# A down projection regrouped: 4 plain chunks, then five groups of a chained 7-product scheme

## The chip, the cores and the metric

The kernel runs on one core of a Trainium2 chip. The metric is the device time of one execution in microseconds (us). A core has TensorE (PE in the profile, with PEld for its weight loads), VectorE (DVE), ScalarE (ACT), GpSimd (POOL) and a queue engine, SyncE (SP), that issues most DMAs. The kernel before took 3144.01 us (median of 3 runs, 3142.61 to 3148.22).

## What is computed

One layer of a hybrid encoder for 640 tokens (512 of a prompt, 8 x 16 of running streams): norm, a combined input projection, gated DeltaNet and sliding-window attention, an output projection, then a ConvFFN. The change touches only the last product:

```python
h2 = rms_norm(x, norm2_w) * (1 + scale2) + shift2
u = h2 @ w_up                                  # 2048 -> 2 x 5632
u_c = causal_dwconv(concat(ffn_prev, u), ffn_conv_w) + ffn_conv_b
gt, up = split(u_c, 2)
x = x + gate2 * ((silu(gt) * up) @ w_down)     # 5632 -> 2048
```

All of it is float32. gate2 is one vector for the prompt and one for each of the 8 streams.

## The kernel before

Features lie on the partitions in chunks of 128, tokens along the free axis: 640 columns in two halves of 320 (HALF), each with 256 columns of the prompt and 64 of four streams. The inner width of 5632 is 44 chunks (NFF), the output 2048 is 16 rows of 128 (KC).

A float32 product is built from three matmuls: each operand x is split into hi (x rounded to float32r, a copy on ACT) and lo = x - hi (a subtraction on DVE), and hi x hi, hi x lo and lo x hi are summed in PSUM. This holds for weights (tiles raw, whi, wlo of 128x512, a unit of four 128x128 blocks) and for activations.

Weights come as a stream of units in a fixed order, which `build_stream` writes down. SP fetches 512 KB at a time into a ring of five buffers (`issue_raw`), `prep_next` forms the sum or difference of two units where one is wanted (tile wsum, a ring of three), `split_next` makes whi and wlo (rings of four), and `next_unit` keeps four units prepared ahead of PE (UB) and the sums two units ahead of those (skew).

Where a group is split, a block product with 2 x 2 blocks (two halves of the features, two halves of the output rows, two halves of the tokens) is made from seven products instead of eight, in ORDER. One job is one value of f, the output rows f and f + 8 together: 7 products of 4 chunks each, 12 matmuls of 320 columns a product. Operand sums are made of weights (five of seven products need one; DPOOL says which GpSimd makes) and of tokens (`mixes`, once a group). The products' sums are formed outside PE: `down(f)` reads every product from PSUM with ACT or DVE, combines them on DVE and GpSimd, and `resid` adds each of the four results to the resident y: one scalar_tensor_tensor on DVE for the 256 prompt columns with gate2, one product into rst on DVE and one addition on GpSimd for the 64 others.

The down projection's 44 chunks go in groups, DGRP: plain 4, split 8, plain 4, split 8, plain 4, split 8, plain 8. In a plain group each of the 16 rows f gets 6 matmuls a chunk (both token halves) and two calls of `resid`. After the last group each row is stored.

Banks: `next_bank` hands out four banks in turn from two PSUM tiles of two banks, named mmd (even) and mm (odd): tile 0 bank 0, tile 1 bank 0, tile 0 bank 1, tile 1 bank 1.

The order of all instructions is written at build time, and every engine runs its own in that order. `Model` keeps an estimated clock for each engine; a side task is a generator in a `Lane`, and `tick`, called after every three or six matmuls, lets lanes go on as long as what they need is ready by that clock. The filling of token operands for the down projection is lane "c" (`chunks`). The gated activations go through DRAM (md): stored by SP chunk by chunk in the up projection, loaded again by GpSimd's queue. The convolution of a pair of up rows is a list of steps that are handed out at SLOTS within the next pair's products; the last pair's come within the first plain group.

Every instruction is recorded at line 90, the wrapper that accounts it, so tiles and not lines tell the operations apart.

Of the kernel before, what the change touches and what calls it, by code (L numbers as in the profile page):

```python
# [6 lines left out]
F32 = mybir.dt.float32  # L7
# [9 lines left out]
ORDER = (2, 4, 5, 1, 6, 7, 3)  # L17
NF = 8
# [14 lines left out]
DGRP = ((0, 4), (1, 8), (0, 4), (1, 8), (0, 4), (1, 8), (0, 8))  # L33
EARLY = 2
DPOOL = {2: 0, 5: 1, 1: 1, 6: 0, 7: 1}
DMIXP = (0, 1, 1, 0, 1)
# [58 lines left out]
class Model:  # L95
    """Estimates when each engine and each tile is free, to order the instructions of parallel tasks."""
# [79 lines left out]
class Ring:  # L176
    """Slots taken in turn, each a tag of a pool."""
# [18 lines left out]
class Slots:  # L196
    """Tiles of any width up to n in the slots of a ring."""
# [30 lines left out]
class Kern:  # L228
# [66 lines left out]
    def add_unit(self, h, *srcs, op=None, pool=False):  # L295
        """Half h (one for all or one each) of one source, or of the sum or difference of two."""
        self.units.append(([k for k, _ in srcs], h if isinstance(h, tuple) else (h,) * len(srcs), op, pool))
        for k, ap in srcs:
            if k not in self.rleft:
                self.rorder.append((k, ap))  # L300
                self.rleft[k] = 0
            self.rleft[k] += 1
# [6 lines left out]
    def build_stream(self):  # L309
# [26 lines left out]
        for split, m in DGRP:  # L336
            for u in range(0 if split else 4 * m):
                self.add_unit(u % 2, (("d", n + u // 2), d["wdn"][n + u // 2]))
            for f in range(8 if split else 0):
                for p in ORDER:  # L340
                    o = OPER[p]
                    src = [(("d", n + 2 * f + j), d["wdn"][n + 2 * f + j]) for j, _ in o[:2]]
                    self.add_unit(tuple(r for _, r in o[:2]), *src, op=o[2] if len(o) > 2 else None, pool=DPOOL.get(p))
            n += 2 * m
# [9 lines left out]
    def prep_next(self):  # L354
        self.issue_raw()
        keys, h, op, pool = self.units[self.apos]
        src = [self.rtile[k][:, i * 512:(i + 1) * 512].rearrange("p (k m) -> p k m", k=4) for k, i in zip(keys, h)]
        if op is not None:
            e = self.nc.gpsimd if pool else self.nc.vector
            t = self.rsum.take([P, 4, P], F32, "wsum")  # L360
            e.tensor_tensor(out=t, in0=src[0], in1=src[1], op=op)
            src = [t]
            self.release(keys)
            keys = ()
        self.ltile[self.apos] = src[0], keys
        self.apos += 1
# [28 lines left out]
    def mm_quarter(self, ps, unit, acts, first, last):  # L395
        nc = self.nc
        hi, lo = unit
        for k, (xh, xl) in enumerate(acts):
            for i, (w, x) in enumerate(((hi, xh), (hi, xl), (lo, xh))):
                nc.tensor.matmul(out=ps, lhsT=w[:, k, :], rhs=x, start=first and k == 0 and i == 0,  # L400
                                 stop=last and k == len(acts) - 1 and i == 2)
# [1050 lines left out]
    def mix_start(self):  # L1452
        """The last gate and the first block of the output projection, as their operands come."""
# [58 lines left out]
    def head(self, h):  # L1512
        """Convolved queries and keys of head h; calling the result gives them with the values."""
# [28 lines left out]
    def phase2(self):  # L1542
# [4 lines left out]
        self.md = tc.dram_tile([NFF, P, NT], F32, name="md")  # L1547
        self.pd = tc.dram_tile([NP, 4, P, HALF], F32, name="pd")
        with tc.tile_pool(name="xres", bufs=1, reuse_waits="tile") as xr, \
# [20 lines left out]
            with tc.tile_pool(name="opx", bufs=1, reuse_waits="tile") as ox:  # L1570
# [3 lines left out]
                with tc.tile_pool(name="ffn", bufs=1, reuse_waits="tile") as fp:  # L1574
                    self.ffn(Tiles(nc, fp, 1))

    def attn_out(self, pa, load):
        """Output projection with its residual, norm, and the first products of NP pairs."""
# [87 lines left out]
    def operand(self, p, j):  # L1666
        """Token operand of product p for the features of chunks j and j + 8, as a sum of two parts."""
# [34 lines left out]
    def pipe(self, ks, ops, s=0, rB=None):  # L1702
        """Steps that scale rows ks, then make the operands ops, a stage of it a step."""
# [45 lines left out]
    def product(self, p, step=None, nh=2):  # L1749
        ps = self.next_bank()  # L1750
        for h in range(nh):
            un = self.next_unit()
            self.feed(self.rate)
            for k in range(4):
                while len(self.ops[p]) <= 4 * h + k:
                    if self.bg:
                        self.feed()
                    else:
# [3 lines left out]
                self.mm_quarter(ps, (un[0][:, k:k + 1], un[1][:, k:k + 1]), [x], h == 0 and k == 0,  # L1762
                                h == nh - 1 and k == 3)
# [4 lines left out]
    def ffn(self, fp):  # L1768
# [18 lines left out]
        def up(i):  # L1787
# [9 lines left out]
            for q, pr in enumerate(ORDER):  # L1797
# [26 lines left out]
                if i == NFF - 1 and q == 3:  # L1824
                    self.lanes["c"].add(chunks())
# [76 lines left out]
        acts, ops, raws, ap, ox = {}, {}, [], self.ap, self.ox  # L1902
        stag = [(ap, f"a{x}{k}") for k in range(6, 16) for x in "hl"] + [(ox, f"ex{k}") for k in range(8)]
        spare = Ring(None, "", 0)
        spare.slots = [[ap, f"a{x}{k}", None] for k in (4, 5) for x in "hl"]
        sums = Slots(spare, NT)

        def raw(c):
            tag = ("ftm", "fext")[len(raws) // 2 % 2]
            raws.append(c)  # L1910
            t = fp.tile([P, 658], F32, tag=tag, name="mraw", bufs=2)[:, 0:NT]
            nc.gpsimd.dma_start(out=t, in_=self.md[c])
            return t

        def whole(c, s, t):
            """Both parts of chunk c, in slot s."""
            tags = [(ap, f"a{x}{s}") for x in "hl"] if s < 4 else stag[2 * s - 8:2 * s - 6]
            hi, lo = (p.tile([P, NT], F32R, tag=n, name=f"m{x}") for x, (p, n) in zip("hl", tags))
            yield (t,)
            nc.scalar.copy(out=hi, in_=t)  # L1920
            yield (hi,)
            v.tensor_tensor(out=lo, in0=t, in1=hi.bitcast(F32), op=ALU.subtract)
            acts[c] = (hi, lo)
            self.done.add(("m", c))

        def mixes(c0, fetch):
            """Token operands of all products for chunks c0 .. c0 + 7, a stage of several at a time."""
            todo, src, hi, low = [(k, q) for k in range(4) for q in range(7)], {}, {}, {}
            for n in range(len(todo) + 3):
                if n < 28:  # L1930
                    k, q = todo[n]
                    if q == 0:
                        while k + 2 > EARLY and self.steps:
                            yield
                        b = [[t[:, s * HALF:(s + 1) * HALF] for s in range(2)] for t in fetch[k]()]
                        (b11, b12), (b21, b22) = b
                        expr = {2: (b11,), 5: (b22,), 4: (b21, b11, ALU.subtract), 1: (b11, b22, ALU.add),
                                6: (b11, b12, ALU.add), 7: (b21, b22, ALU.add), 3: (b12, b22, ALU.subtract)}
                        yield b21, b11
                    x = expr[ORDER[q]]  # L1940
                    src[n] = x[0]
                    if len(x) > 1:
                        src[n] = sums.tile([P, HALF], F32, "", "msum")
                        e = nc.gpsimd if DMIXP[q - 1 - (q > 2)] else v
                        e.tensor_tensor(out=src[n], in0=x[0], in1=x[1], op=x[2])
                if 0 <= n - 1 < 28:
                    k, q = todo[n - 1]
                    yield (src[n - 1],)
                    pool, tag = stag[4 * q + k]
                    t = pool.tile([P, NT], F32R, tag=tag, name="mop")  # L1950
                    hi[n - 1], low[n - 1] = t[:, 0:HALF], t[:, HALF:NT]
                    nc.scalar.copy(out=hi[n - 1], in_=src[n - 1])
                m = n - 2
                if 0 <= m < 28:
                    yield (hi[m],)
                    v.tensor_tensor(out=low[m], in0=src[m], in1=hi[m].bitcast(F32), op=ALU.subtract)
                    ops[c0][ORDER[todo[m][1]]].append((hi[m], low[m]))

        def chunks():
            c0, ts = 0, []  # L1960
            for c in range(4):
                ts.append(ap.tile([P, NT], F32, tag=f"ah{c + 8}", name="mraw"))
                nc.gpsimd.dma_start(out=ts[c], in_=self.md[c])
            for g, (split, m) in enumerate(DGRP):
                if split:
                    ops[c0] = {p: [] for p in ORDER}
                    rs, early = [], EARLY if g == 1 else 0

                    def get(k):
                        if k < early:  # L1970
                            rs.append([stag[18 - 4 * k + j][0].tile([P, NT], F32, tag=stag[18 - 4 * k + j][1], name="mraw")
                                       for j in range(2)])
                            for j in range(2):
                                nc.gpsimd.dma_start(out=rs[k][j], in_=self.md[c0 + k + 4 * j])
                        else:
                            rs.append((raw(c0 + k), raw(c0 + k + 4)))

                    for k in range(max(1, early)):
                        get(k)

                    def fetch(k):
                        while len(rs) < min(k + 2, 4):
                            get(len(rs))
                        return rs[k]

# [216 lines left out]
```

## Time and profile before

| | |
|---|---|
| timed runs | 3142.61, 3144.01, 3148.22 us |
| profiled execution, first to last instruction (span) | 3137.7 us; its time with what lies around the span isn't shown |
| PE busy | 2974.9 us, 95%, 19841 matmuls |
| DVE busy | 2319.3 us, 74% |
| ACT busy | 1195.7 us, 38% |
| GpSimd busy | 1147.2 us, 37% |
| DMA | 428.32 MB, 137 GB/s on average |
| mean granted clock of TensorE | 0.983 of 2.4 GHz |

Busy time is the union of an engine's instructions. Matmuls are pipelined: a row gives 0.31 us for a matmul of 320 columns, but the next one starts before that is over, so the pace is read from start to start or from many in a row. The same holds for DVE: an operation's duration is some 0.08 us longer than the distance to the start of the next. The up projection fills PE from about 1600 us to 2484 us, and the down projection is the rest.

### The profile page before, as it was taken

How to read it: one execution, taken by the hardware profiler on the slowest of the kernel's cores; microseconds unless marked ns; L12 is line 12 of the kernel's file. 1: busy time of each engine (PE TensorE's matmuls, PEld its weight loads, DVE VectorE, ACT ScalarE, POOL GpSimd, SP SyncE). 2: the span in 40 equal slices, each digit the busy share in tenths (PEclk: the TensorE clock that was granted, in tenths of full speed). 3: DMA queues.
4: the chain of work that ended last, by engine and by line, in shares of the span. 5: the costliest groups of instructions: out<-in, count | busy, mean ns of one | idle time of the engine just before them, and what ended most of it. 6: DMA issues, size and time to landing. Idle time of an engine off the chain costs nothing. (4 is left out here: it accounts for less than half of the span.)

```text
span 3137.7 us, 53459 instructions
## 1 busy us (share of the span) xinstructions
PE 2974.9 (95%) x19841; PEld 2795.6 (89%) x19841; DVE 2319.3 (74%) x4513; ACT 1195.7 (38%) x2245; POOL 1147.2 (37%) x1665
## 2 busy tenths in 40 slices
PE   6999999999999999987999999999999988999898
PEld 2688889899999978876899999999999988989898
DVE  4333437778886424798889899889999899999962
ACT  2432334333442312553444444444444433333321
POOL 2210013233422311465333333333333466666631
PEclk8999989999999999999999999999999999999999
DMA  8755533222223788546433333333333532323232
GB/s 339 283 182 182 176 116 85 78 75 90 79 80 114 254 296 293 165 148 207 140 110 99 96 101 102 102 106 96 101 101 97 176 136 81 115 81 111 90 102 74
DMA packets 189988, 428.32 MB, mean 137 GB/s; under 512 B 49778, under 2 KB 77968, under 8 KB 189712
## 3 DMA queue, kind: packets, MB, share of 16 engines
q1 hardware_dynamic: 152000, 362.15, 35.1%
q0 software_dynamic: 14960, 51.51, 4.8%
q10 hardware_dynamic: 22768, 11.25, 1.4%
q8 instruction: 156, 2.56, 0.3%
q14 instruction: 104, 0.85, 0.1%
HBM read 381.70 MB, written 44.96 MB: 136 GB/s over the span
## 5 line engine op out<-in xcount | busy, mean ns | idle before, releaser
L90 DVE TENSOR_TENSOR wlo<-raw,whi 128x512 fp32r<-128x512 f32 x576 | 446.0, 779 | 317.7 <-ACT whi L90 290.9
L90 ACT CAST whi<-raw 128x512 fp32r<-128x512 f32 x576 | 353.1, 619 | 526.5 <-PE mm L90 361.0
L90 ACT CAST whi<-wsum 128x512 fp32r<-128x512 f32 x560 | 342.4, 619 | 348.0 <-PE mm L90 102.2
L90 DVE TENSOR_TENSOR wlo<-wsum,whi 128x512 fp32r<-128x512 f32 x560 | 435.8, 779 | 22.1 <-ACT whi L90 19.3
L90 PE MATMUL mm<-mh,wlo 128*128 128x320 f32 x1536 | 431.8, 312 | 10.0 <-DVE wlo L90 9.9
L90 PE MATMUL mm<-mh,whi 128*128 128x320 f32 x1536 | 431.2, 311 | 8.2 <-DVE qsq L90 6.6
L90 PE MATMUL mm<-ml,whi 128*128 128x320 f32 x1536 | 430.1, 310 | 0.0
L90 DVE TENSOR_TENSOR wsum<-raw 128x512 f32<-128x512 f32 x463 | 369.1, 797 | 81.9 <-DMA raw<-in_wup 77.8
L90 PE MATMUL mm<-hh,wlo 128*128 128x320 f32 x1376 | 330.6, 322 | 7.6 <-DVE wlo L90 7.6
L90 PE MATMUL mm<-hh,whi 128*128 128x320 f32 x1376 | 327.5, 319 | 4.6 <-ACT hh L90 3.2
L90 PE MATMUL mm<-hl,whi 128*128 128x320 f32 x1376 | 327.0, 319 | 0.6 <-DVE hl L90 0.6
L90 PEld LDWEIGHTS mm<-mh,wlo 128*128 128x128 f32 x1536 | 277.0, 188 | 23.9 <-DVE wlo L90 12.1
L90 PE MATMUL mmd<-mh,wlo 128*128 128x320 f32 x1024 | 292.1, 311 | 6.1 <-DVE wlo L90 6.1
L90 PEld LDWEIGHTS mm<-mh,whi 128*128 128x128 f32 x1536 | 277.6, 188 | 19.0 <-issue 7.1
L90 PE MATMUL mmd<-ml,whi 128*128 128x320 f32 x1024 | 292.0, 310 | 2.4 <-DVE ml L90 2.3
L90 PE MATMUL mmd<-mh,whi 128*128 128x320 f32 x1024 | 292.1, 311 | 0.5 <-ACT qacc L90 0.5
L90 PEld LDWEIGHTS mm<-ml,whi 128*128 128x128 f32 x1536 | 277.4, 189 | 6.9 <-issue 6.7
L90 PEld LDWEIGHTS mm<-hh,wlo 128*128 128x128 f32 x1376 | 230.7, 191 | 21.2 <-issue 11.0
L90 PEld LDWEIGHTS mm<-hh,whi 128*128 128x128 f32 x1376 | 230.1, 191 | 21.7 <-issue 12.8
L90 PEld LDWEIGHTS mm<-hl,whi 128*128 128x128 f32 x1376 | 230.2, 190 | 19.6 <-issue 16.5
L90 POOL TENSOR_TENSOR y<-y,rst 128x64 f32<-128x64 f32 x224 | 122.2, 545 | 208.5 <-DVE rst L90 206.0
L90 PEld LDWEIGHTS mmd<-mh,wlo 128*128 128x128 f32 x1024 | 186.7, 189 | 7.7 <-DVE wlo L90 7.7
(426 smaller groups left out, 6491.7 us busy)
## 6 DMA issues: line engine op xcount, KB each, us to landing
raw<-in_wup SPq DMA_DIRECT2D x206, 512.0 KB, 3.7
araw<-in_adaw SPq DMA_DIRECT2D x256, 256.0 KB, 5.1
raw<-in_wdn SPq DMA_DIRECT2D x88, 512.0 KB, 3.5
raw<-in_win SPq DMA_DIRECT2D x82, 512.0 KB, 3.7
araw<-in_adaw SPq DMA_DIRECT2D x64, 512.0 KB, 6.4
raw<-in_wo SPq DMA_DIRECT2D x48, 512.0 KB, 5.7
mraw<-md POOLq DMA_DIRECT2D x44, 320.0 KB, 4.6
md<-ftm SPq DMA_DIRECT2D x44, 256.0 KB, 5.3
```

The costliest lines, as they stand in the source:

```text
L90: return f(*args, **kw)
```

## The change

DGRP becomes plain 4 and then five split groups of 8. The split scheme becomes one with 4 + 4 operand sums, whose results share partial sums: product 1 is followed in the same PSUM bank by products 6, 7 and 4, and product 5 by product 3 (ONTO), so a bank holds one sum after the other and each is added to one block of y as it stands. Two of the weight sums are kept and used in the next ones; GpSimd makes one a job (product 7), DVE the three others. `product` gets the bank and whether it starts it.

y is now the ungated sum of the down projection and lies in DRAM (yd). The plain group writes it (a copy by ACT from PSUM, then a store). Each job then loads its two rows (640 columns each), adds the seven sums on DVE, one addition of 320 columns each, and stores them; loads go one job ahead, into two pairs of buffers. Only the last group loads x, applies `resid` and stores the result. The token operands of a group are made by `fill`, two chunks at a time (640 columns), from four loads on SP's queue, into slots that come free as the group before uses its operands for the last time. The steps of the last pair's convolution are all handed out at the end of the up projection.

```diff
+WINO = (1, 5, 6, 2, 7, 3, 4)
+ONTO = {6: 1, 7: 1, 4: 1, 3: 5}
-DGRP = ((0, 4), (1, 8), (0, 4), (1, 8), (0, 4), (1, 8), (0, 8))
-EARLY = 2
-DPOOL = {2: 0, 5: 1, 1: 1, 6: 0, 7: 1}
-DMIXP = (0, 1, 1, 0, 1)
+DGRP = ((0, 4),) + ((1, 8),) * 5
+DPOOL = {7: 1}
...
-                for p in ORDER:
-                    o = OPER[p]
...
+                a = [[(("d", n + 2 * f + j), d["wdn"][n + 2 * f + j], r) for r in range(2)] for j in range(2)]
+                t = {k: (("s", n + 2 * f, k), None, 0) for k in (5, 6)}
+                for p, src, op in ((1, (a[0][0],), None), (5, (a[1][0], a[1][1]), ALU.add),
+                                   (6, (t[5], a[0][0]), ALU.subtract), (2, (a[0][1],), None),
+                                   (7, (a[0][0], a[1][0]), ALU.subtract), (3, (a[0][1], t[6]), ALU.subtract),
+                                   (4, (a[1][1],), None)):
...
-    def product(self, p, step=None, nh=2):
-        ps = self.next_bank()
+    def product(self, p, step=None, nh=2, ps=None, first=True):
+        ps = self.next_bank() if ps is None else ps
...
+        while self.steps:
+            self.steps.pop(0)[1]()
+
+    def fill(self, dp, c0, key):
...
+        def put(p, t):
+            slot, user = self.slots.pop(0)
+            while user is not None and user not in self.done:
+                yield
+            self.slots.append((slot, ("p", key, p)))
...
+        for d in range(2):
+            b = {}
+            for n, (r, s) in enumerate(((0, 0), (0, 1), (1, 1), (1, 0))):
+                b[r, s] = ox.tile([P, 2, HALF], F32, tag=f"ex{4 + n}", name="mq")
+                k = c0 + 4 * r + 2 * d
+                nc.sync.dma_start(out=b[r, s], in_=self.mdt[k:k + 2, :, s * HALF:(s + 1) * HALF].rearrange(
+                    "k p c -> p k c"))
+            t1, t2, t3, t4 = (dp.tile([P, 2, HALF], F32, tag="stg", name=f"t{n + 1}", bufs=4) for n in range(4))
+            yield from put(1, b[0, 0])
+            yield (b[0, 1],)
+            v.tensor_tensor(out=t1, in0=b[0, 1], in1=b[0, 0], op=ALU.subtract)
+            yield from put(5, t1)
...
+    def down(self, dp):
...
+            y = ox.tile([P, 2, HALF], F32, tag=f"ex{f % 4}", name="y0")
+            nc.scalar.copy(out=y, in_=ps[:, :, 0:HALF])
...
+        for n in range(njobs):
+            f, g = n % 8, n // 8
+            last = g == len(DGRP) - 2
+            if f == 0 and not last:
+                lane.add(self.fill(dp, DGRP[0][1] + 8 * (g + 1), g + 2))
...
+            a, b = self.main_ps2(0)[0], self.main_ps2(1)[0]
+            banks = {1: a[:, 0, 0:HALF], 2: b[:, 0, 0:HALF], 5: b[:, 1, 0:HALF]}
+            for q, pr in enumerate(WINO):
+                ps = self.product(pr, None, 1, banks[ONTO.get(pr, pr)], pr not in ONTO)
+                if f == 7:
+                    self.done.add(("p", g + 1, pr))
+                r, h = dest[pr]
+                y = ys[n][r][:, h]
+                v.tensor_tensor(out=y, in0=y, in1=ps, op=ALU.add)
+                if q == 1:
+                    tail()
+                if q == 3 and n + 1 < njobs:
+                    ys[n + 1] = load(n + 1)
+                if q == 1 and last:
...
+                if last and q > 2:
+                    k = f + 8 * r
+                    self.resid(dp, "rst", x[r][:, h], y, 5, k, h)
+                    late.append(lambda x=x[r][:, h], k=k, h=h: nc.sync.dma_start(
+                        out=self.o["yT"][:, k, h * HALF:(h + 1) * HALF], in_=x))
+            if not last:
+                late.append(lambda n=n, ts=ys.pop(n): store(n, ts))
+        tail()
```

`tail` issues what is in `late`: the stores of the job before. The first bank tile is mm or mmd in the names of the trace as before; `fill`, `down` and the pool "dn" come after the up projection's pool is closed.

## Rows read from the trace of the kernel before

**Rows 1.** The page's busy times: us, share of the span, instructions
```profile
PE 2974.9 (95%) x19841; PEld 2795.6 (89%) x19841; DVE 2319.3 (74%) x4513; ACT 1195.7 (38%) x2245; POOL 1147.2 (37%) x1665
```

**Rows 2.** Stretches: length, busy us of PE, PEld, DVE, ACT, POOL; clock, DMA share, GB/s
```profile
1600.00:2470.00 870.00, 870.00 (x5934) 870.00 (x5933) 786.43 (x1305) 404.09 (x672) 294.33 (x479) 1.00 0.32 100
2484.33:2541.51 57.18, 56.58 (x387) 56.32 (x385) 49.41 (x109) 21.50 (x42) 38.31 (x60) 1.00 0.67 232
2541.51:2666.71 125.20, 106.39 (x675) 101.36 (x674) 120.98 (x192) 43.85 (x82) 85.80 (x88) 0.97 0.26 85
2666.71:2723.03 56.32, 56.32 (x387) 56.32 (x386) 52.69 (x121) 21.29 (x45) 39.09 (x59) 1.00 0.38 131
2723.03:2840.17 117.14, 104.95 (x674) 101.33 (x673) 112.54 (x176) 41.55 (x76) 77.64 (x79) 0.97 0.24 80
...
2896.49:3013.90 117.41, 105.23 (x675) 101.61 (x673) 110.57 (x176) 41.41 (x76) 78.62 (x81) 0.97 0.25 85
3013.90:3127.75 113.85, 113.06 (x770) 112.53 (x768) 43.18 (x100) 20.52 (x33) 18.12 (x35) 1.00 0.28 93
3127.75:3137.70 9.95, 0.00 (x0) 0.00 (x0) 1.23 (x4) 0.00 (x0) 0.64 (x2) 0.70 0.09 33
```

**Rows 3.** The chain of waits in the last plain stage: start, us, what
```profile
3092.54 7.04 PE mm L90 x48
```

**Rows 4.** PE's waits in the second split stage: total us, times, longest
```profile
PE mmd L90 <- DVE t L90: 4.8, 3, 2.8
PE mm L90 <- ACT t L90: 2.6, 3, 1.0
```

**Rows 5.** DVE in order of time, third split stage: start, duration, operation
```profile
2902.83 0.68 DVE L90 TENSOR_TENSOR wlo<-wsum,whi 128x512 fp32r<-128x512 f32 x1
2903.43 0.81 DVE L90 TENSOR_TENSOR ml<-mraw,mh 128x640 fp32r<-128x640 f32 x1
2904.16 0.68 DVE L90 TENSOR_TENSOR wlo<-raw,whi 128x512 fp32r<-128x512 f32 x1
...
2908.59 0.48 DVE L90 TENSOR_TENSOR t<-mmd,e 128x320 f32<-128x320 f32 x1
2908.99 0.47 DVE L90 SCALAR_TENSOR_TENSOR y<-c,mod,y 128x256 f32<-128x256 f32 x1
2909.39 0.21 DVE L90 TENSOR_TENSOR rst<-c,mod 128x64 f32<-128x64 f32 x1
2909.52 0.68 DVE L90 TENSOR_TENSOR wlo<-raw,whi 128x512 fp32r<-128x512 f32 x1
...
2910.53 1.64 DVE L90 TENSOR_TENSOR wsum<-raw 128x512 f32<-128x512 f32 x1
2912.09 1.35 DVE L90 TENSOR_TENSOR wlo<-wsum,whi 128x512 fp32r<-128x512 f32 x1
```

**Rows 6.** GpSimd in order of time, the same stretch
```profile
2910.34 1.27 POOL L90 TENSOR_TENSOR wsum<-raw 128x512 f32<-128x512 f32 x1
```

**Rows 7.** PE in order of time, two waits in split stages (in brackets)
```profile
2736.52 0.87 PE L90 MATMUL mmd<-mop,whi 128*128 128x320 f32 x2 [2.77 <-DVE t L90]
...
2909.22 0.53 PE L90 MATMUL mmd<-mop,whi 128*128 128x320 f32 x2 [2.00 <-DVE t L90]
```

**Rows 8.** Busy time and granted clock right after the first of these waits
```profile
2735.00:2744.00 9.00, 7.48 (x32) 7.51 (x33) 9.00 (x17) 0.86 (x2) 5.51 (x7) 0.62 0.15 55
```

**Rows 9.** DVE in order of time at the start of the first plain stage
```profile
2492.77 0.48 DVE L90 SCALAR_TENSOR_TENSOR y<-mmd,mod,y 128x256 f32<-128x256 f32 x1 [4.84 <-DMA y<-xd]
```

**Rows 10.** DMA issues: queue, count, KB each, median us from issue to landing
```profile
raw<-in_wdn SPq DMA_DIRECT2D x88, 512.0 KB, 3.5
araw<-in_adaw SPq DMA_DIRECT2D x64, 512.0 KB, 6.4
mraw<-md POOLq DMA_DIRECT2D x44, 320.0 KB, 4.6
md<-ftm SPq DMA_DIRECT2D x44, 256.0 KB, 5.3
```

More of the change, by code (lines that the diff above doesn't have):

```diff
@@ L362, in prep_next @@
             src = [t]
+            if keep is not None:
+                self.rtile[keep] = t
             self.release(keys)
@@ L393, in next_unit, with mm_quarter @@
         return u
-    def mm_quarter(self, ps, unit, acts, first, last):
+    def mm_quarter(self, ps, unit, acts, first, last, kw={}):
         nc = self.nc
@@ L1575, in phase2 @@
                     self.ffn(Tiles(nc, fp, 1))
+                with tc.tile_pool(name="dn", bufs=1, reuse_waits="tile") as dp:
+                    self.down(Tiles(nc, dp, 1))
     def attn_out(self, pa, load):
@@ L1824, in up @@
                 if i == NFF - 1 and q == 3:
-                    self.lanes["c"].add(chunks())
+                    self.lanes["c"].add(first_chunks())
             conv(i, ext)
@@ L1900, in conv @@
             self.steps += sorted(zip(SLOTS2 if i + 1 < NP else SLOTS, fns), key=lambda x: x[0])
[L1902 to L1984, printed above, removed]
-                    while g > 1 and ("g", g - 2) not in self.done:
-                        yield
-                    yield from mixes(c0, [lambda k=k: fetch(k) for k in range(4)])
-                else:
-                    if g:
-                        ts = [raw(c0 + s) for s in range(4)]
-                    for s in range(m):
-                        while g > 1 and ("g", g - 2 + s // 4) not in self.done:
-                            yield
-                        yield from whole(c0 + s, s, ts[s])
-                        if s + 4 < m:
-                            ts.append(raw(c0 + s + 4))
-                c0 += m
@@ new lines, in ffn, with first_chunks @@
+        ap = self.ap
+        self.acts, raws = {}, {}
+        def first_chunks():
+            n = DGRP[0][1]
+            for c in range(n):
+                raws[c] = ap.tile([P, NT], F32, tag=f"ah{n + c}", name="mraw")
+                nc.sync.dma_start(out=raws[c], in_=self.md[c])
+            for c in range(n):
+                hi, lo = (ap.tile([P, NT], F32R, tag=f"a{x}{c}", name=f"m{x}") for x in "hl")
+                yield (raws[c],)
+                nc.scalar.copy(out=hi, in_=raws[c])
+                yield (hi,)
+                v.tensor_tensor(out=lo, in0=raws[c], in1=hi.bitcast(F32), op=ALU.subtract)
+                self.acts[c] = (hi, lo)
+                self.done.add(("m", c))
@@ L2037, in ffn @@
-        for k in range(3):
-            load(k)
-        c0 = slot = self.nbank = 0
-        for g, (split, m) in enumerate(DGRP):
-            if split:
-                while c0 not in ops:
-                    self.pump()
-                self.ops = ops[c0]
-                for f in range(8):
-                    down(f)
-            for f in range(0 if split else KC):
-                if g == 0 and 0 < f < KC - 2:
-                    load(f + 2)
-                ps, pv = self.main_ps2(f)
-                for u in range(0, m, 4):
-                    step(slot)
-                    slot += 4
-                    un = self.next_unit()
-                    for k in range(4):
-                        c = c0 + u + k
-                        self.until(("m", c))
-                        self.wait(*acts[c])
-                        self.mm_unit(pv, (un[0][:, k:k + 1], un[1][:, k:k + 1]), [acts[c]], u + k == 0, u + k == m - 1)
-                for i in range(2):
-                    self.resid(fp, "t2", xs[f][i], pv[i], 5, f, i)
-                    if g == len(DGRP) - 1:
-                        nc.sync.dma_start(out=self.o["yT"][:, f, i * HALF:(i + 1) * HALF], in_=xs[f][i])
-            self.done.add(("g", g))
-            c0 += m
```

123 lines of the change are left out of this document (81 added, 42 removed).

## Prediction

> **What bounds the kernel now.** I read the page's busy table first [rows 1]: PE is busy in 95% of the span and DVE in 74%, but averages hide the stages, so I cut the span into stages by the matmuls' operands and read the busy time of each [rows 2]. Up to 2484 us PE is busy without a gap while DVE runs at 90%; the change leaves all of that as it is. The down projection is the rest, from the first matmul on an mh tile at 2484.33 to the last one's end at 3127.75: 643.4 us. It is four plain stages (57.2, 56.3, 56.3 and 113.8 us) and three split ones (125.2, 117.1 and 117.4 us), and they have different limits. In a plain stage PE has no gaps: in the chain of waits 48 matmuls of 320 columns take 7.04 us, so one takes 0.1467 us [rows 3]. A split stage has 8 x 7 x 4 x 3 = 672 matmuls, 98.6 us at that pace, and takes 16 to 27 us more. There DVE is the busy engine, 112.5 of 117.1 us in the second stage, and PE waits for DVE's readings of PSUM and for ACT's copies that stand behind them [rows 2, 4]. The split job (one value of f) takes 359.8/24 = 15.0 us, where its 84 matmuls need 12.32.
>
> So two things can give time: fewer matmuls, at 0.1467 us each, and the 64 us that the three split stages lose to DVE (359.8 less 3 x 98.6).
>
> **Matmuls.** Before: 20 plain chunks x 16 rows x 6 = 1920 and 3 x 672 = 2016, together 3936. After: 4 x 16 x 6 = 384 and 5 x 672 = 3360, together 3744. The 192 that go are 28.2 us. At full pace the new down takes 56.3 + 40 jobs x 12.32 = 549.1 us, 94.3 less than now. Everything below decides how much of that is lost again.
>
> **DVE in a new job.** Each job has 7 low parts of 128x512 and 3 weight sums of 128x512 on DVE (products 5, 6 and 3; the sum for 7 is GpSimd's) and 7 additions of 128x320 from PSUM into y. The starts of undisturbed DVE operations lie 0.60 us apart for 512 columns, 0.73 for 640, 0.40 for 320 or for the 256-column residual, 0.13 for its rst [rows 5]. So a job is 10 x 0.60 + 7 x 0.40 = 8.8 us. The filling of a group's operands adds, in two halves, 2 x (4 sums + 7 low parts) = 22 operations of 640 columns, 16.2 us, and some 0.3 for the slots made of four tiles: 16.5 a group, 2.1 a job. Now a job has 9 weight operations, 5 of 320 columns, 4 residuals with rst and 1.8 us of filling, about 11.4 undisturbed; the change takes away the residuals (4 a job now, only in the last group afterwards) and one sum on balance goes to DVE, so the raw load falls by 0.5 us, to 10.9.
>
> The larger part is disturbance. Beside GpSimd's additions a weight sum of DVE takes 1.64 us and a low part 1.35, where a low part alone takes 0.68 [rows 5, 6]; a reading of PSUM keeps its 0.48. GpSimd is busy 77.6/8 = 9.7 us a job now [rows 2], with three weight sums, three sums of products, four additions for rst; afterwards one weight sum (and in the last group four short additions). I bound one such sum's cost to DVE by 0 (it falls beside additions from PSUM) and 0.96 us (1.64 less 0.68), and take 0.75, near the rows that collide. New job: 10.9 + 0.75 = 11.65 us of DVE against 12.32 of PE. On average PE is the bound again, with 5% to spare. ACT is no candidate: 41.6 us of 117 now, and it loses its PSUM copies in the jobs.
>
> **The wait that decides.** The additions are new waits in both directions. DVE's addition of product q waits for PE, and DVE works in order: behind it stand the low parts of the weights three products ahead, which PE has 5.3 us to wait for. In return, products 6, 7 and 4 add onto product 1's bank and 3 onto 5's, so PE may not start them before DVE has read what is there. Between lies one other product, 12 x 0.1467 = 1.76 us. Now the same sort of wait is seen: PE sits 2.00 us before the third product's matmuls until DVE's t is done at 2909.07 [rows 5, 7]. By the order in which the code hands out banks that reading is of the other bank of the same tile, so the wait goes by tile: products 2 and 3 wait so too, for 5 and 2. From 1.76 I take 0.2 until DVE starts after PE, 0.48 for the addition and 0.15 back to PE (2909.07 to 2909.22): DVE may be 0.9 us late, and beyond that each 0.1 stalls PE by 0.1.
>
> The Trainium skill ("PSUM — Partial Sum Buffer", § PSUM bank collisions raise a hardware error) says that two engines keep out of each other's way by bank and quadrant, and that other banks may be used at once. By that products 2 and 3 would not wait for 5 and 2, and if five tight waits share the 22 us of stalls that I find in the jobs below, two fifths of them would go: an estimate of 3071 us, within my own case. The trace doesn't agree as far as this kernel goes: the 2.00 us above are a wait on the other bank.
>
> **Stalls, term by term.** (a) Groups 1 to 4, where the next group is filled: low end 0, spread evenly (11.65 < 12.32); high end, all filling in two jobs, 2 x 9.55 + 16.5 = 35.6 against 24.6, 11 us a group. The filling is handed out a step at a time, each when the planner's clock has its source ready, and the last four of 14 operands wait for slots freed in job 8; so it comes over four to five jobs and then in the last. Five jobs at 9.55 + 3.1 = 12.7, with bursts of two or three operations (1.5 to 2.2 us) over the 0.9 allowed: I take 4 us a group, 16. (b) Entry to the first group: the first y comes back from DRAM only after the last store and ACT's copy. Low end 0, high end the 4.84 us for which DVE waited for y<-xd at the start of down [rows 9]; I take 3. After a wait of 2.77 us in the second split stage the granted clock was 0.62 on average over 9 us, so in the lower of its two levels, 1.2 GHz, for most of them [rows 7, 8]; that lost 9 x 0.38 = 3.4 us. I add it once: 6.4; the high end is 8.2. (c) Last group: no filling, but 4 residuals (0.40 + 0.13) a job: 8.8 + 2.1 + 0.75 = 11.7, GpSimd's short additions beside it, and x is fetched only one and a half products before its use. Low 0, high 1.5 us a job (12); I take 6. (d) Entry to the plain stage: the last pair's convolution steps are all issued before it rather than spread over it; DVE has four taps of 656 columns (0.75 at the pace of [rows 5]) and two products with waits for GpSimd and ACT between, some 8 us, covered by three prepared units of 24 matmuls, 10.6. Low 0, high 5; I take 2. (e) The end: 9.95 us from the last matmul to the end of the span now, with two residuals; one addition, one residual and four stores then. Same.
>
> Sum: 549.1 + 16 + 6.4 + 6 + 2 = 579.5, 63.9 less than 643.4. The profiled span of 3137.7 becomes 3073.8. The median of the timed runs is 6.3 above that span (3144.01), which I take as what lies around it: **3080 us**. All low ends: 3050; all high ends (44, 8.2, 12, 5): 3119.
>
> **DMA.** A job moves 2 weight loads of 512 KB, 2 y loads and 2 stores of 320 KB and a share of the filling, about 2.7 MB, in 12.3 us: near 215 GB/s, where the second split stage has 80 at a share of 0.24 and the first plain stage 232 at 0.67 [rows 2]. The 44 loads of md [rows 10] also leave GpSimd's queue for SP's; GpSimd has room either way. The weights have five buffers, over two jobs' worth. Tight is y: SP sends the old y's store about 1.7 us into a job, the next load waits in the same buffers for it, and behind that on SP stand the next weights. With 3.5 to 5.3 us a transfer [rows 10] the store is done at 5 to 7, the load sent at about 7.2 (after the weights' fetch, which waits for a low part) and landed by 11 to 13; it is needed at 12.3 + 1.8 = 14.1. Filling loads (4 x 320 KB, some 4 us) reach into this twice a group; that is part of (a).
>
> **Rivals.** *PE at full pace.* DVE keeps within 0.9 us nearly everywhere, as it kept up at 90% in the up projection [rows 2]: stalls under 10 us, 3050 to 3060. Against it: there the banks gave several products of slack. 10%.
> *The round trip of y decides.* If transfers at this load take the 6.4 us that the 512 KB loads of the start took [rows 10], store and load end at 14.5 and the second y at 15.4; with the filling in between, DVE then stands before y. Every us beyond the 0.9 in every job costs 40: 3100 to 3140, 3120 for one. 20%.
> *Lockstep, slower than before.* [...] If a new job takes the 15.0 us of an old one, down takes 40 x 15.0 + 56.3 + 6 = 662 us, 19 more: 3163. It is slower from 14.5 us a job, (643.4 - 62)/40, that is 2.2 us of stall in each. For it: the same waits, five of seven products. Against: DVE's own load is 11.65 and not 14, so it would have to stand idle 3 us a job. 6%.
>
> **Numbers.** My case, stalls of 10 to 50 us (3060 to 3100), has 60%; 4% is left near no change, between the last two. Range for 8 in 10: 3053 to 3114, which drops part of the first rival, the upper half of the second and the third. What a measurement can tell is 0.2%, 6 us. Faster by more: 0.91; within: 0.03; slower: 0.06.
>
> **What would show it.** Right: plain stage 56 to 59 us; jobs of groups 1 to 4 at 12.5 to 13, DVE busy over 90% there with low parts near 0.68, GpSimd under 15%; PE's waits released by DVE's y, each under 1.5 us, and granted clock 1.0 but for the first job. Wrong: DVE waiting for DMA y<-yd in most jobs (second rival), or jobs over 14 us with waits on y before five of seven products (third).

## The result, and the profile after

The changed kernel takes 3095.66 us (median of 4 runs, 3092.89 to 3098.09) against 3143.72 for the kernel before (4 runs, 3142.61 to 3148.22). The ratio is 0.9849, with a 95% interval of 0.9835 to 0.9862: 1.5% faster. The forecast was 3080, with a range of 3053 to 3114.

The page's busy times [rows 1], now:

```profile
PE 2943.2 (95%) x19649; PEld 2765.0 (89%) x19649; DVE 2291.0 (74%) x4419; ACT 1225.0 (40%) x2255; POOL 843.9 (27%) x1283
```

The 192 matmuls fewer are there (19841 to 19649), and the shares of PE and DVE have not moved at all: averages hide this change. The same stretches as in [rows 2] show it: the plain group, the five split groups and the end (length, busy us of PE, PEld, DVE, ACT, POOL; clock, DMA share, GB/s).

```profile
2491.32:2547.64 56.32, 56.32 (x386) 56.32 (x385) 37.22 (x54) 30.17 (x50) 3.73 (x8) 1.00 0.64 221
2547.64:2654.04 106.40, 100.55 (x675) 98.58 (x673) 94.50 (x162) 44.85 (x77) 11.34 (x8) 1.00 0.62 206
2654.04:2762.42 108.38, 102.34 (x674) 100.10 (x673) 94.89 (x164) 44.27 (x76) 10.52 (x8) 0.98 0.59 199
2762.42:2867.20 104.78, 99.54 (x674) 98.55 (x673) 95.40 (x162) 43.72 (x72) 11.82 (x8) 1.00 0.62 206
2867.20:2974.18 106.98, 100.64 (x674) 98.56 (x673) 94.75 (x167) 44.46 (x78) 10.63 (x8) 1.00 0.61 202
2974.18:3090.46 116.28, 101.77 (x674) 98.47 (x672) 96.40 (x194) 32.92 (x53) 29.16 (x38) 1.00 0.53 183
3090.46:3096.20 5.74, 0.00 (x0) 0.00 (x0) 1.11 (x3) 0.00 (x0) 0.32 (x1) 0.83 0.16 57
```

Down now takes 599.1 us (2491.32 to 3090.46) instead of 643.4. Groups 1 to 4 take 105 to 108 us each where a split group took 117 to 125; GpSimd's busy time in one falls from 78 to 86 us to about 11. The last group takes 116.3 us, with 29.2 on GpSimd. A group's 672 matmuls need 98.56 us at full pace, so the five groups lose 7.8, 9.8, 6.2, 8.4 and 17.7 us, together 50. Those 50 us are what has to be explained: 28 were forecast (terms a, b and c).

The two spans differ by 41.5 us: 44.3 less in down, 4.2 less at the end (5.74 for 9.95), and 7.0 more ahead of down, which starts at 2491.32 and not at 2484.33. The 7.0 us are there before the up projection fills PE: the 9501st matmul starts at 1544.93 us before and at 1551.85 after, and the change touches nothing so far ahead. In the eight kernels below, which share that part, down starts between 2483.6 and 2489.9, so most of it is the difference from one execution to the next.

PE's waits in groups 1 to 4 (total us, times, longest):

```profile
PE mmd L90 <- DVE y L90: 15.3, 18, 2.0
PE mm L90 <- DVE y L90: 5.7, 6, 1.2
PE mmd L90 <- ACT whi L90: 1.2, 2, 0.7
PE mm L90 <- ACT whi L90: 1.1, 2, 0.5
```

PE waits almost only for DVE's additions into y, as forecast; the waits for ACT's t of [rows 4] are gone. From here on, stalls are given by the product that PE stands before, read from matmul start to matmul start. Over the whole of down PE loses 17.3 us before product 4, 15.9 before 6, 5.2 before 3, 3.4 before 7 and 3.0 before 2: exactly the five that have to wait for an addition. Jobs beside which no filling goes on (the sixth and seventh of a group) take 12.32 us, with no stall at all.

**What a stall in groups 1 to 4 looks like.** The fourth job of group 2 takes 17.15 us. DVE in order of time (start, duration, operation, in brackets the idle time before it and what ended it):

```profile
2697.22 0.49 DVE L90 TENSOR_TENSOR y<-y,mmd 128x320 f32<-128x320 f32 x1 [1.81 <-PE mm L90]
2697.62 0.68 DVE L90 TENSOR_TENSOR wlo<-wsum,whi 128x512 fp32r<-128x512 f32 x1
2698.22 0.82 DVE L90 TENSOR_TENSOR dop<-mq,dop 128x640 fp32r<-128x640 f32 x1
2698.96 0.82 DVE L90 TENSOR_TENSOR t<-mq 128x640 f32<-128x640 f32 x1
2699.70 0.48 DVE L90 TENSOR_TENSOR y<-y,mm 128x320 f32<-128x320 f32 x1
...
2701.09 1.67 DVE L90 TENSOR_TENSOR wsum<-raw 128x512 f32<-128x512 f32 x1
...
2704.89 0.88 DVE L90 TENSOR_TENSOR dop<-t,dop 128x320 fp32r<-128x320 f32 x2
2705.69 0.81 DVE L90 TENSOR_TENSOR t<-mq 128x640 f32<-128x640 f32 x1
2706.54 0.82 DVE L90 TENSOR_TENSOR t<-t,mq 128x640 f32<-128x640 f32 x1
2707.28 0.48 DVE L90 TENSOR_TENSOR y<-y,mmd 128x320 f32<-128x320 f32 x1
```

And PE's waits in that stretch:

```profile
2697.85 0.53 PE L90 MATMUL mmd<-dop,whi 128*128 128x320 f32 x2 [0.65 <-ACT whi L90]
2700.32 0.53 PE L90 MATMUL mm<-dop,whi 128*128 128x320 f32 x2 [0.48 <-DVE y L90]
2707.91 0.38 PE L90 MATMUL mmd<-dop,whi 128*128 128x320 f32 x1 [2.00 <-DVE y L90]
```

The addition at 2707.28 has two half operations and two full ones of the filling (dop, t, t) in front of it, 2.4 us in one piece; PE stands 2.00 us for it and starts at 2707.91, right behind it. At 2698.22 another such pair (dop, t) stands in front of the addition at 2699.70, and so PE waits again. In between one weight sum takes 1.67 us beside GpSimd's sum. The first row shows DVE idle for 1.81 us; its releaser is named as PE, but the matmuls of that product had made way to the next at 2695.28. What came last is y's own load: on SP it is issued at 2691.12, behind four loads of the filling.

```profile
2689.05 1.98 SPq L90 DMA_DIRECT2D mq<-md  x4
2691.12 0.92 SPq L90 DMA_DIRECT2D y<-yd  x2
```

**And in the last group.** DVE's waits there, then PE's:

```profile
DVE xo L90 <- DMA xo<-xd: 10.8, 6, 2.3
```

```profile
PE mmd L90 <- DVE y L90: 14.5, 13, 1.7
```

DVE in order of time, in its third job:

```profile
3003.43 1.28 DVE L90 SCALAR_TENSOR_TENSOR xo<-y,mod,xo 128x256 f32<-128x256 f32 x1
3004.64 0.21 DVE L90 TENSOR_TENSOR rst<-y,mod 128x64 f32<-128x64 f32 x1
3004.77 0.68 DVE L90 TENSOR_TENSOR wsum<-raw,wsum 128x512 f32<-128x512 f32 x1
3005.37 0.81 DVE L90 TENSOR_TENSOR wlo<-raw,whi 128x512 fp32r<-128x512 f32 x1
3006.11 0.47 DVE L90 TENSOR_TENSOR y<-y,mmd 128x320 f32<-128x320 f32 x1
...
3013.26 0.49 DVE L90 SCALAR_TENSOR_TENSOR xo<-y,mod,xo 128x256 f32<-128x256 f32 x1 [2.25 <-DMA xo<-xd]
```

Two things are seen. At 3013.26 the first residual of a job waits 2.25 us for x, which SP issues at 3008.65 behind the stores of the job before; the addition behind the residual comes late, and PE stands before product 4 (8.8 us over the group, and 9.5 to 10.7 in the kernels below that leave this as it is; before product 6 it is 7.8). And at 3003.43 a residual stands in front of the low part and the addition at 3006.11; it takes 1.28 us where its fellow takes 0.49, because GpSimd's weight sum runs at 3003.14 for 1.30 us. PE stands 0.98 us before product 6.

### The profile page after: what moved, and what is told of

It reads as the page before. It is cut to its first block, busy times and chain, and to the rows that moved or that the text cites. A ratio compares the mean times of both kernels' runs of the same rounds, so it can differ in the third digit from the quotient of the medians.

```text
span 3096.2 us, 52887 instructions
## 1 busy us (share of the span) xinstructions
PE 2943.2 (95%) x19649; PEld 2765.0 (89%) x19649; DVE 2291.0 (74%) x4419; ACT 1225.0 (40%) x2255; POOL 843.9 (27%) x1283
## 4 chain that ended last, share of the span: by engine, by line
PE 41%; DVE 6%; DMA 3%; issue 2%; SPq 1%; POOL 0%; ACT 0%; DVEq 0%; POOLq 0%; ACTq 0%
PE mmd L90 21%; PE mm L90 19%; DVE wlo L90 2%; DVE y L90 1%; DVE dop L90 1%; DMA xo<-xd 1%; DVE wsum L90 1%; SPq L90 1%; DMA fext<-pd 1%; DMA y<-yd 1%; DVE t L90 1%; DVE ftm L90 0%; DMA e<-pd 0%; DVE xo L90 0%; DMA yd<-y 0%
## 5 line engine op out<-in xcount | busy, mean ns | idle before, releaser
L90 PE MATMUL mm<-mh,wlo 128*128 128x320 f32 x1280 | 374.2, 313 | 10.1 <-DVE wlo L90 10.0
L90 PE MATMUL mm<-mh,whi 128*128 128x320 f32 x1280 | 373.8, 312 | 9.3 <-DVE qsq L90 8.1
L90 PE MATMUL mm<-ml,whi 128*128 128x320 f32 x1280 | 372.9, 312 | 0.6 <-DVE ml L90 0.6
L90 PE MATMUL mmd<-dop,whi 128*128 128x320 f32 x1280 | 287.2, 312 | 31.2 <-DVE y L90 29.8
L90 PEld LDWEIGHTS mm<-mh,whi 128*128 128x128 f32 x1280 | 235.4, 189 | 20.5 <-issue 7.1
L90 PEld LDWEIGHTS mm<-hh,whi 128*128 128x128 f32 x1376 | 230.7, 191 | 21.9 <-issue 13.7
L90 PEld LDWEIGHTS mmd<-dop,whi 128*128 128x128 f32 x1280 | 213.8, 189 | 39.1 <-ACT whi L90 25.7
L90 PEld LDWEIGHTS mm<-ml,whi 128*128 128x128 f32 x1280 | 235.2, 189 | 7.8 <-issue 6.7
L90 PE MATMUL mmd<-mh,wlo 128*128 128x320 f32 x768 | 233.2, 310 | 6.5 <-DVE wlo L90 6.5
L90 PE MATMUL mmd<-mh,whi 128*128 128x320 f32 x768 | 233.0, 310 | 1.1 <-ACT qacc L90 1.1
L90 PE MATMUL mmd<-ml,whi 128*128 128x320 f32 x768 | 232.7, 310 | 0.5 <-DVE ml L90 0.4
```

Of the source, the lines that this page charges most:

```text
L90: return f(*args, **kw)
```

## The experiments

The theory after the result was that each of the 50 us is a DVE addition that comes late for its own reason: filling in bursts, x late, residuals in front. The rivals were a chip limit (DVE's load as a whole, the collision with GpSimd, DMA traffic) and the choice of PSUM tiles. The experiments are called e1 to e8, in the order below. Each starts from the changed kernel, and its time is the median of 4 runs; the ratio is to the kernel before, run beside it (median of 7 runs: 3146.21 us for e1 to e4, 3142.72 for e5 to e8). The changed kernel's ratio was 0.9849.

### x a job earlier

```diff
-                if q == 1 and last:
+                if last and (q == 1 and f == 0 or q == 3 and f < 7):
+                    fx = f + (q == 3)        # loads x of job fx
...
```

> Only the last group's loads of x move: from the second product of the same job to the fourth product of the job before (the first job keeps its place). Theory A (x lands too late, DVE stands before its first residual, and product 4 waits for the addition of 7 behind it): the 2.3 us waits of DVE for DMA xo<-xd and PE's 1.4 to 1.9 us before product 4 go, those of 1.15 us before product 6 stay; last group 116.3 -> 107 to 108 us, time 3095.7 -> about 3087. Rival B (DVE has too much to do in the last group, with 4 residuals and GpSimd beside it): the waits only change their name, the group stays at 114 to 117.

3082.7 us, ratio 0.9797 [0.9770, 0.9823]. The last group, and PE's waits in it:

```profile
2967.39:3073.87 106.48, 100.58 (x674) 98.45 (x672) 96.42 (x194) 32.93 (x53) 29.19 (x38) 1.00 0.61 200
```

```profile
PE mmd L90 <- DVE y L90: 5.9, 8, 1.0
```

116.3 becomes 106.5 with the same DVE work (96.4 us busy in both). The stalls before product 4 fall from 8.8 to 0.5 us; those before 6 stay, 6.7 for 7.8. So the late x makes the larger of the two kinds of stall.

### The residuals behind the next addition

```diff
-                    self.resid(dp, "rst", x[r][:, h], y, 5, k, h)
+                    pend.append((x[r][:, h], y, k, h))
...
                 v.tensor_tensor(out=y, in0=y, in1=ps, op=ALU.add)
+                add_x()                      # resid and store for what is in pend
```

> Only the order on DVE in the last group changes: each residual comes after the next product's addition into y instead of before it (that of product 4 after the next job's product 1). The work is the same. Theory C (what costs is that additions on which the next product waits stand behind residuals, whose scalar_tensor_tensor collides with GpSimd or waits for x): the 1.15 us before product 6 go, and most of those before 4, since the addition of 7 no longer stands behind the wait for x; last group 101 to 106 us, time about 3082 to 3086. Rival B (DVE's load): 114 to 117, no change. If x alone were the cause (A without C), DVE would still wait as long and the group would stay above 108.

3084.56 us, 0.9807 [0.9784, 0.9831].

```profile
2970.40:3073.33 102.93, 100.36 (x674) 98.46 (x672) 94.08 (x192) 32.94 (x53) 29.17 (x37) 1.00 0.61 205
```

This alone takes the last group to 102.9, 13.4 us less and more than e1: only 3.7 us of stalls are left, before 6. It also takes off the stalls before 4: one product later x has nearly always landed, and DVE's waiting for it falls from 10.8 to 2.1 us. So late x cost time only by the additions that stood behind the waiting residual.

### No filling

```diff
-                lane.add(self.fill(dp, DGRP[0][1] + 8 * (g + 1), g + 2))
+                self.dops[g + 2] = self.dops[1]
```

> Leaves out the operands of groups 2 to 5: no loads of md, no sums, copies and low parts for them; all five groups use the operands of group 1, so the output is another one. Theory D (groups 1 to 4 lose their 32 us to the filling alone): every job of groups 1 to 4 takes 12.32 us but the first (14 to 15), each of these groups 98.6 to 101, together 427 -> 397 us; time about 3066. Rival E (the chained sums and GpSimd's weight sum cost by themselves, filling or not): the groups stay above 103 each, time above 3080.

3064.23 us, 0.9739 [0.9720, 0.9757]. Groups 1 and 2; 3 and 4 are as 2:

```profile
2542.94:2643.38 100.44, 98.79 (x675) 98.56 (x673) 78.58 (x134) 35.48 (x57) 10.42 (x8) 1.00 0.59 192
2643.38:2741.94 98.56, 98.56 (x675) 98.56 (x673) 79.96 (x136) 34.91 (x56) 10.42 (x8) 1.00 0.59 193
```

Groups 2 to 4 run at PE's full pace to the hundredth, with every wait for an addition, y's way through DRAM and GpSimd's sum still in place. All of term (a) belongs to the filling, and the entry costs 1.9 us without it (the first job, 14.20). DVE's load is 80/8 = 10.0 us a job without the filling and 11.9 with it, on average over a group; where in the group it falls is shown under e7.

### The filling without its loads

```diff
-            b = {}
+            if key > 1:
+                b = self.bq                  # the tiles of the first filling, no DMA
+            else:
+                b = self.bq = {}
...
```

> Leaves out the DMA loads of the filling for groups 2 to 5 (4 x 320 KB twice a group); ACT's and DVE's work of the filling stays and is done on the tiles of group 1's second half, so the output is another one. Theory F (the filling costs by bursts on DVE): the two long jobs, the fourth of groups 2 and 4 (17.2 and 16.6 us), where y<-yd comes late behind these loads, fall to 13 to 14, the rest stays; groups 1 to 4 together 427 -> 417 to 421, time 3086 to 3090. Rival G (the filling costs by its DMA, through late y and late operands): groups 1 to 4 at 400 to 408, time about 3070 to 3077.

3092.82 us, 0.9828 [0.9809, 0.9847]. The four groups take 106.7, 106.4, 106.0 and 106.2 us, together 425.3 against 426.5. The two jobs of over 16 us are gone, but the stalls turn up elsewhere (3.3 us before product 3 in each of groups 2 to 4). I had expected 417 to 421, and 3086 to 3090 us for the whole. The edit did more than it was meant to: the steps of the filling are placed at build time by when their sources are ready, and without loads to wait for they stand in other jobs. In DVE's order, group 2's eight jobs have 5, 6, 6, 2, 0, 0, 0 and 9 operations of the filling up to the last addition of each, where the changed kernel has 5, 5, 1, 6, 2, 0, 0 and 9. So this run shows that the loads alone are not what the filling costs, but not what they cost.

### The sum for product 7 on DVE

```diff
-DPOOL = {7: 1}
+DPOOL = {}
```

> The one weight sum that GpSimd makes in a job (product 7) goes to DVE. Theory H (a sum on GpSimd costs DVE about as much in collisions, 0.7 us, as it costs when DVE makes it, 0.6): groups 1 to 4 together within 5 us of 427, the last within 4 us of 116.3, the residual's scalar_tensor_tensor at 0.48 instead of 1.28 us beside the sum; time 3091 to 3100. Rival I (GpSimd's sum is nearly free for DVE): DVE has 0.6 us a job more in the jobs that are full already, groups 1 to 4 rise by 12 to 20 us, time over 3105.

3091.89 us, 0.9836 [0.9821, 0.9851]. DVE's residuals in the last group, first with GpSimd's sum, then without it (mean ns behind the busy time):

```profile
L90 DVE SCALAR_TENSOR_TENSOR xo<-y,mod,xo 128x256 f32<-128x256 f32 x31 | 20.7, 666 | 11.7 <-DMA xo<-xd 10.8
```

```profile
L90 DVE SCALAR_TENSOR_TENSOR xo<-y,mod,xo 128x256 f32<-128x256 f32 x32 | 15.5, 485 | 12.6 <-DMA xo<-xd 11.6
```

The collision is gone, 666 to 485 ns, and DVE has eight more sums a group; its busy time in groups 1 to 4 together rises only from 379.5 to 381.6 us. The groups take 105.3, 105.8, 104.0, 107.4 and 116.8 us, the first four together 422.5 for 426.5. Of the 32 x 0.60 = 19.2 us that 32 more sums take, DVE gets 17.1 back: a sum on GpSimd cost it 0.53 us, nearly as much as doing it.

### A PSUM tile for each of the three banks

```diff
+            banks = {}
...
+                if pr not in ONTO:
+                    banks[pr] = self.main_ps2(nt[0])[0][:, 0, 0:HALF]
+                    nt[0] += 1
```

> Products 2 and 5 no longer share a PSUM tile: a job takes three tiles of the four in turn instead of two, so that product 2 need not wait for the addition of 5 nor 3 for that of 2, but product 5 of the next job waits for the addition of 4. Theory J (waits go by tile): PE's stalls before products 2 and 3 (3.0 and 5.2 us in the whole of down) go; some of them come back before 4 and 5; time down by 2 to 7 us, 3089 to 3094. Rival K (waits go by bank): stalls before 2 and 3 stay where they are; no change, or a few us more from the new wait.

3105.82 us, 0.9876 [0.9862, 0.9891]. Group 4, and PE's waits in groups 1 to 4:

```profile
2871.25:2980.15 108.90, 102.82 (x674) 101.65 (x673) 95.88 (x167) 44.38 (x78) 11.88 (x8) 0.97 0.59 198
```

```profile
PE mmd L90 <- DVE y L90: 13.2, 8, 2.8
PE mm L90 <- DVE y L90: 13.0, 13, 2.1
```

The stalls before 2 and 3 are gone (8.2 us in the changed kernel's down, 0.1 now). That shows that a wait goes by tile, as this program sets its waits: the bank is another one either way. But I had expected 3089 to 3094 us, and groups 1 to 4 take 434.8 instead of 426.5: PE now stands before products 4 and 7, in fewer and longer waits (up to 2.8 us for 2.0), and the granted clock falls to 0.97 and 0.98 on average in three of the four groups, where that happened in one. PEld's busy time for the same loads gives its size: 98.56 us undisturbed, 100.1 in groups 2 and 3, 101.65 in group 4, so 6.2 us over four groups against 1.6 in the changed kernel. From one matmul to the next inside the products, it is 3.7 of the 8.3 us by which the groups are longer.

The rest lies in the waits, and for that the edit has a second effect, as in e4: the filling is placed otherwise, in group 2 with 5, 6, 6, 2, 0, 0, 0 and 9 operations to a job, and DVE is busy for up to 15.8 us within one job (14.6 in the changed kernel). What it has beyond PE's 12.32 us in single jobs grows from 15.2 to 23.9 us over the four groups, about as much as they do. So the run doesn't show what the tiles are worth by themselves.

### The filling paced

```diff
-                lane.add(self.fill(dp, DGRP[0][1] + 8 * (g + 1), g + 2))
+                filler.append([self.fill_paced(dp, DGRP[0][1] + 8 * (g + 1), g + 2), None, 0])
...
                 if q == 3 and n + 1 < njobs:
                     ys[n + 1] = load(n + 1)
+                pace(q)   # one DVE step of the filling at most, after the additions of products 1, 5, 7 and 3;
+                          # its loads only here, behind y's
```

> The filling for groups 2 to 5 does the same operations in another rhythm: one DVE operation at a time, right after the addition of product 1, 5, 7 or 3 (those after which DVE makes no weight sum next), ACT's copies one a product, loads only behind the next y's load. Theory F (what costs is that operations come in bursts of two or three, while DVE's mean load of 11.65 us a job leaves room): groups 1 to 4 at 99 to 102 us each, 427 -> 397 to 406, as with no filling but for the first job; the last group unchanged; time 3066 to 3076. Rival L (DVE's load, however it is spread): groups 1 to 4 stay over 103 each, time over 3083.

3069.12 us, 0.9762 [0.9746, 0.9778]. The four groups take 101.3, 100.4, 99.3 and 101.4 us, together 402.4. The third:

```profile
2747.93:2847.26 99.33, 99.03 (x674) 98.55 (x673) 95.06 (x163) 44.03 (x72) 10.39 (x8) 1.00 0.65 218
```

The third group has DVE busy for 95.06 us, the changed kernel for 95.40; the same operations, and it is done in 99.3 us and not 104.8. The DMA moves more a second, not less. So it is not DVE's load in the whole group, nor the traffic. But the edit changes two things: one step of the filling stands between two additions, and the filling is spread over nearly all jobs. Job by job, DVE's load is not the same (third group; job length, busy us of PE, PEld, DVE and so on). The changed kernel's second, fourth, sixth and eighth jobs:

```profile
2774.74:2789.98 15.24, 12.83 (x86) 12.32 (x85) 14.63 (x25) 7.38 (x13) 1.30 (x1) 1.00 0.63 208
...
2802.30:2816.59 14.29, 12.55 (x86) 12.31 (x85) 13.99 (x23) 5.61 (x9) 1.76 (x1) 1.00 0.62 209
...
2828.91:2841.23 12.32, 12.32 (x86) 12.32 (x85) 9.99 (x17) 4.36 (x7) 1.30 (x1) 1.00 0.58 192
...
2853.55:2867.20 13.65, 12.56 (x86) 12.32 (x85) 13.32 (x22) 6.96 (x11) 1.79 (x1) 1.00 0.52 174
```

And e7's third, fourth and sixth:

```profile
2772.57:2784.90 12.33, 12.33 (x87) 12.32 (x85) 12.33 (x22) 5.70 (x10) 1.30 (x1) 1.00 0.56 176
2784.90:2797.63 12.73, 12.55 (x86) 12.32 (x85) 12.73 (x22) 6.87 (x11) 1.30 (x1) 1.00 0.57 191
...
2809.95:2822.27 12.32, 12.32 (x86) 12.32 (x85) 10.89 (x19) 5.00 (x8) 1.30 (x1) 1.00 0.87 306
```

In the changed kernel DVE is busy for 14.63, 13.99 and 13.32 us in three jobs of this group, more than the 12.32 that PE needs, and for 9.99 in two others; in e7 the fullest job has 12.73. Over groups 1 to 4, 13 jobs of the changed kernel have DVE busy beyond 12.32, by 15.2 us together, in e7 4.6. So about half of what the filling costs is DVE's load within single jobs, the rival that e7 left open, and only the rest can be the order inside a job or late loads. e7 can't tell these apart.

### All together

The paced filling, x a job earlier, the residuals behind the next addition, and the first y loaded ahead of the plain group's last store.

> The paced filling, x loaded a job ahead, residuals one product later, and the first y loaded before the last row of the plain group is done, all together. If the causes are separate and add: groups 1 to 4 at 98.6 to 101 each (the first without its wait for y), the last at 99 to 103, down 56.3 + 395 to 404 + 101 = 553 to 562 us instead of 599, time 3050 to 3062. If one limit (DVE's load) is behind all of them, a part of the gains is lost together: over 3065.

3055.58 us (3052.80 to 3058.02), 0.9720 [0.9705, 0.9735]. The second and the last group, and all of PE's waits in the split groups:

```profile
2645.24:2745.42 100.18, 99.50 (x675) 98.56 (x674) 95.12 (x164) 44.42 (x76) 10.38 (x8) 1.00 0.65 215
...
2944.00:3045.20 101.20, 100.35 (x674) 98.45 (x672) 94.75 (x194) 32.96 (x53) 29.20 (x37) 1.00 0.63 209
```

```profile
PE mm L90 <- DVE y L90: 1.2, 5, 0.3
```

The five groups take 500.0 us, with a floor of 492.8: the 50 us are 7. In groups 1 to 4 the gains add, 24.1 by the paced filling and 1.9 in the first job by the earlier y, of 27.7 in all. In the last group they overlap: e1 takes off 9.8, e2 13.4, both together 15.1. And a limit by DVE's load is still there: 4.4 of the 4.6 us that groups 1 to 4 lose are in jobs in which DVE is never idle, of up to 12.87 us. This version is faster than both kernels, 40 us below the changed one by the medians.

## Why the prediction was right, and where it was off

**Right in mechanism.** The matmuls fell as counted, 28.2 us. The bound went from DVE back to PE on average over a group: DVE's busy time in a job of groups 1 to 4 is 11.9 us on average (forecast 11.65), in the last group 96.4/8 = 12.05 (11.7), GpSimd's share is 11%. The new waits lie on DVE's y, before five products, and the two that only share a tile wait too (e6), as the trace of before had it [rows 7]; by the Trainium skill ("PSUM — Partial Sum Buffer", § PSUM bank collisions raise a hardware error) alone, they would not have had to. The first rival (under 10 us of stalls) fell; e8 shows it to be within reach. The second (y through DRAM in every job) fell: in groups 2 to 4 of e3 y goes the same way and costs nothing. Its loads and stores land after 3.8 and 4.9 us, in the 3.5 to 5.3 that [rows 10] suggested:

```profile
yd<-y SPq DMA_DIRECT2D x80, 320.0 KB, 4.9
y<-yd SPq DMA_DIRECT2D x80, 320.0 KB, 3.8
```

Lockstep fell: a job of groups 1 to 4 takes 426.5/32 = 13.3 us, not 15.0.

**Mis-sized: (a), the filling, 16 forecast and 29.7 measured** (32.3 in groups 1 to 4, less 2.6 for the entry). e3 alone gives 30.4. The step that was too small is the 4 us a group. The prediction had five jobs with 12.7 us of DVE work, 0.4 over PE's 12.32, and put bursts on top. Measured, the filling stands in fewer and fuller jobs: the 13 jobs that go beyond 12.32 have DVE busy for 13.5 us on average, 14.6 at most, 15.2 us over in all. The fourth jobs of groups 2 and 4 are 6.1 us longer than DVE's work in them; there y comes late behind the filling's loads, which the prediction had named as a part of (a). The other 8.4 us lie in the rest of the jobs; the rows of the fourth job above show the kind, an addition behind two or three steps in a row. What a burst costs by itself no run shows: e7 removes most of all three at once.

**Mis-sized: (c), the last group, 6 forecast and 17.7 measured,** above my high end of 12. "x is fetched only one and a half products before its use" stood there as a remark, without a price; it makes 9.8 us of the 17.7 (e1). It does so only through the residual that waits for x in front of an addition: with the residual one product later and x as late as before, 13.4 us go (e2). And the residuals' collision with GpSimd's sum was left out: [rows 5] has a residual at 0.47 us and I took that for the kind, though only the weight operations there had GpSimd beside them. Beside a sum it takes 1.28.

**Smaller.** (b) The entry cost 2.6 us and not 6.4 (1.9 without the filling, e3): PE's wait was 1.54 us, and the granted clock of group 1 stayed at 1.00 on average. (d) The plain group cost nothing (56.32) instead of 2. (e) The end took 5.74 us instead of 9.95; nothing was tried on that. The 6.3 us between span and median are not what lies around an execution: 1.8 us are (3097.97 less 3096.2), and 2.1 in the later runs of the kernel before; the rest is that the profiled execution of before was a short one. Two readings were loose and enter no sum: PE has no gap from 1600 us on [rows 2], not all the way up to 2484, and the split stages take 18.5 to 26.6 us over 98.6, not 16 to 27. The 22 operations of the filling at 0.73 us are 16.1 us and not 16.2.

The sum: 13.7 (a) + 11.7 (c) - 3.8 (b) - 2.0 (d) = 19.6 us more in down than forecast. With -4.2 at the end, +7.0 ahead of down and -4.5 around the span the profiled execution comes to 3097.9 from 3080; it was 3097.97.

## What to carry to other kernels

Where PE waits for an engine that works in order, ask two things: what stands in front of each operation that PE waits for, and how much that engine has to do in each short stretch, not only on average. With the same 95 us of DVE work, a group took 104.8 us when single jobs held up to 14.6 us of it, and 99.3 when none held more than 12.7. In the last group the load was not what mattered: the same 96.4 us of DVE work took 116.3 us or, with x loaded a job earlier, 106.5. So spread side work by count over all jobs, one step between two awaited operations, and put what nobody waits for (a residual, a store) behind the next awaited operation, where a late load cannot hold it up. A remark in a forecast ("x is fetched late") wants a price: work out when it is issued, when it lands, and what is queued behind its user.

## What was not expected of the hardware

A DVE scalar_tensor_tensor of 128x256 with its inputs in SBUF takes 1.28 us beside a GpSimd sum and 0.49 alone; the additions that read PSUM kept their 0.48 throughout. A GpSimd sum of 128x512 cost DVE 0.53 us, where the sum itself takes DVE 0.60 (e5), so having one such sum there bought nothing. In e6, with waits of up to 2.8 us, the granted clock fell in three groups of four, and that was 3.7 of the 8.3 us by which they grew.
